# A hybrid state-space and delta-rule layer: four inverses around the GLU, an output projection in three parts, and high parts on ScalarE

## Chip, cores and metric

The kernel runs on one core of a Trainium2 chip. The metric is the device time of one execution in microseconds, the median of several runs.

## What is computed

One layer on 1024 latent tokens and 256 context tokens of width 1024. An input projection is split between two groups of heads. The S5 group is a two-way diagonal state-space scan with GELU, a GLU and a SiLU gate; the other is a gated delta rule with four heads of 128, in chunks of 64 tokens, both ways. Both are concatenated, projected, gated and normalised with the residual. Cut to what the change touches:

```python
h = x * (1.0 + scale[:, None]) + shift[:, None]
u, z_s5, qkv, z_gdn, beta_l, alpha_l = jnp.split(h @ p['w_in'], _proj_splits(), axis=-1)
...
g = jax.nn.gelu(y, approximate=False)                          # S5: y is the scan's read-out
s5 = g * jax.nn.sigmoid(g @ w_glu + b_glu) * jax.nn.silu(z)
...
sol = lax.linalg.triangular_solve(a_mat + eye, rhs, left_side=True, lower=True, unit_diagonal=True)
...
def step(s, inp):
    qi, ki, ui0, wi, qki, gi, gli = inp
    u = ui0 - wi @ s
    o = gi * (qi @ s) + qki @ u
    s = gli * s + ki.T @ u
    return s, o
...
y = jnp.concatenate([s5_lat, gdn_lat], axis=-1) @ w_out
x_new = _layer_norm(DEEPNORM_ALPHA * x + gate[:, None] * y, p['ln_g'], p['ln_b'])
```

## The kernel before

The kernel is written with tile pools and a list scheduler: the order in which the code is written gives priorities, and the scheduler settles, when the kernel is built, the order of the instructions on each engine. On the chip each engine goes through its own list in that order. A tile of a pool whose memory is still in use makes its first writer wait.

Matrices of float32 are multiplied in three passes (`mm3`, lines 140 to 143): both factors are split into a high and a low part, and low by high, high by low and high by high are added in PSUM. A 128x512 tile of a product of depth 128 is three matmuls. `split` (lines 874 to 876) makes the parts: ScalarE copies the high part, VectorE subtracts for the low one.

The work goes through these stages.

- Prologue (to about 90 us): the modulation from c and w_ada, h (tiles `h_hi`, `h_lo`, eight of 128x1024; `c_hi`, `c_lo` for the context) and the S5 input `u` (`u_mm`, line 499), with masks `lvm` for the inverse made on VectorE (line 1078).
- The projections of q, k and v with their convolutions, head by head, and beside them the S5 scan's states. Then a list written by hand, `ORD`, orders: eight z projections (`z0` to `z7`, 48 matmuls of 128x512 each, tiles `pjz`), four pairs of Toeplitz tiles (`t0` to `t3`), four read-outs (`y0` to `y3`: `y_stage`, tiles `py`, then transposes `pg` and the GELU tile `gT`), the GLU's weights (`w`) and the GLU (`g`: 96 matmuls `pgl`, then sigmoid on ScalarE, products on VectorE, stores to `d_mix`). `>y0` behind a name holds that item back until y0 is done.
- 20 inverses, for 4 heads in 5 batches of 256 tokens each (batch 4 is the context). `tbatch` builds one: decay sums `pd`, products `pkk`, the masked parts on GpSimd (`mg`, `dec`, `thi`, `tlo`, `xz`, `r`), a recursion of doubling block sizes in which TensorE (`pz`, `pp`, `px`), VectorE (`pad`, `xz`) and ScalarE alternate, and its result `pzz`. Its `finish` makes `zf` (ScalarE) and `ks` (GpSimd, from the load `kt`). Two of them are traced ahead of the others, next to the preparation of the first half of the output weights, `wo_a` (`load_wo`: load of a row `wor`, product with the gate on GpSimd or VectorE, split).
- For each head a scan of 10 chunk steps in both directions (`scan_head`, tiles `s`, `rr`, `uu`, `st`, sums in `acc`), then the gated norm.
- The output projection in two parts. `part_out` (heads of S5, k 0 to 3, 192 matmuls `poa`) is a generator; `fill` takes three matmuls of it at a time between the steps of an inverse or a scan. It adds alpha x and stores the sum in DRAM (`d_y`). When it is drained, after batch 16, `wo_b` is loaded into the memory of `wo_a`. `out_tile` then multiplies k 4 to 7 for each of 8 tiles of 128 tokens (192 matmuls `pout`), adds the stored sum (line 1553), and normalises: squares on ScalarE, scaling on VectorE (line 1568), the last addition on GpSimd or VectorE (lines 1570 to 1575). Tile `m7` is the part that comes from the last head's scan; the other three come back through DRAM (`load_mix`).

Loads and stores sit mostly on SP's queue, in order; some stores are issued by ScalarE.

## Time and profile before

| | |
|---|---|
| median of 3 runs | 914.95 us (912.2 to 919.06) |
| profiled execution | 909.83 us |
| its span, first to last instruction | 907.9 us |
| TensorE matmul busy, instructions | 808.6 us (89%), 6553 |
| VectorE busy | 681.8 us (75%), 1330 |
| ScalarE busy | 403.3 us (44%), 874 |
| GpSimd busy | 388.5 us (43%), 463 |

The profiled execution is one run; its 909.83 us hold the span of 907.9 and 1.9 us around it. In the rows PE is TensorE, DVE is VectorE, ACT is ScalarE, POOL is GpSimd, SP the queue that issues most loads; L and a number is a line of the kernel before. `x` and a number counts instructions. PEclk is the clock granted to TensorE as a share of its full speed. TensorE's matmuls overlap, so that a matmul shown with 0.39 us may start 0.23 us after the one ahead of it.

### The profile page before, as it was taken

The numbers are of one execution on the slowest core, as the hardware profiler recorded it, in microseconds if no ns is written. First come the engines' busy times: TensorE is split into PE (matmuls) and PEld (weight loads), VectorE is DVE, ScalarE is ACT, GpSimd is POOL, SyncE is SP. The second block draws the span as 40 slices with busy tenths as digits, with TensorE's granted clock in tenths as the row PEclk, the third lists the DMA queues.
The fourth block names the chain that finished last, engine by engine and source line by source line (L and its number), as shares of the span: only waits on it lengthen the run. The fifth ranks groups of instructions, "written<-read, shape, count | busy, mean of one in ns | idle before, by whom it ended". The sixth has DMA issues, their size and how long they took to land. (4 is left out here: it accounts for less than half of the span.)

```text
span 907.9 us, 17108 instructions
## 1 busy us (share of the span) xinstructions
PE 808.6 (89%) x6553; PEld 671.6 (74%) x6553; DVE 681.8 (75%) x1330; ACT 403.3 (44%) x874; POOL 388.5 (43%) x463
## 2 busy tenths in 40 slices
PE   4988999999897989999897894899989999888994
PEld 2756897787786668887786673688978887777883
DVE  7889986998877767998763389567685684775586
ACT  1232435234433344423433365566763573564363
POOL 3216240006999920001111078774963773351063
PEclk9989999999999999999898997799999999799998
DMA  9981547501314431444434477321234324324332
GB/s 246 302 157 49 196 158 232 152 24 47 133 47 157 128 122 47 134 131 137 138 115 123 147 263 228 127 83 59 64 118 149 118 92 158 110 77 150 111 127 105
DMA packets 120124, 119.48 MB, mean 132 GB/s; under 512 B 21406, under 2 KB 95702, under 8 KB 119914
## 3 DMA queue, kind: packets, MB, share of 16 engines
q1 hardware_dynamic: 101946, 85.42, 33.1%
...
q14 instruction: 31, 0.25, 0.1%
HBM read 81.33 MB, written 37.04 MB: 130 GB/s over the span
## 5 line engine op out<-in xcount | busy, mean ns | idle before, releaser
L713 POOL TENSOR_TENSOR rta<-ebuf,ar 128x64 f32<-128x64 f32 x38 | 25.9, 682 | 86.0 <-DVE ebuf L688 83.2
L846 POOL COPY hq<-ebuf 64x1024 f32<-64x1024 f32 x8 | 16.0, 2016 | 106.8 <-issue 60.6
L143 PE MATMUL pjz<-h_hi,wtz 128*128 128x512 f32 x128 | 51.5, 402 | 0.0
L141 PE MATMUL pjz<-h_hi,wtz 128*128 128x512 f32 x128 | 51.5, 402 | 0.0
L142 PE MATMUL pjz<-h_lo,wtz 128*128 128x512 f32 x128 | 51.4, 402 | 0.0
L1297 PEld LDWEIGHTS <-xz 128*128 128x128 f16 x480 | 37.4, 101 | 18.4 <-issue 12.1
L1186 POOL TENSOR_TENSOR mg<-tri,ghi 128x512 fp32r<-128x512 f32 x20 | 22.5, 1124 | 65.3 <-PE pd L1194 33.4
L1281 DVE TENSOR_TENSOR pad<-pp,lvm 128x256 f16<-128x256 f32 x100 | 40.7, 417 | 8.9 <-PE pp L1273 8.4
L1297 PE MATMUL px<-pad,xz 128*128 128x64 f16 x480 | 42.8, 197 | 4.8 <-DVE pad L1281 3.6
L1310 DVE TENSOR_TENSOR xz<-px,xz 128x512 f16<-128x512 f32 x60 | 40.6, 684 | 6.9 <-PE px L1297 6.5
L759 DVE SCALAR_TENSOR_TENSOR cav<-crv,cwt,cav 128x945 f32<-128x945 f32 (+2 forms) x32 | 39.6, 1238 | 6.0 <-ACT cav L749 5.5
L1297 PE MATMUL px<-xz,pad 128*128 128x64 f16 x480 | 43.0, 197 | 0.0
L759 DVE SCALAR_TENSOR_TENSOR cak<-crk,cwt,cak 128x945 f32<-128x945 f32 (+2 forms) x32 | 39.6, 1238 | 1.4 <-ACT cak L749 1.0
L759 DVE SCALAR_TENSOR_TENSOR caq<-crq,cwt,caq 128x945 f32<-128x945 f32 (+2 forms) x32 | 39.4, 1231 | 1.0 <-ACT caq L749 0.4
L1273 PE MATMUL pp<-xz,t 128*128 128x64 f16 x480 | 34.1, 198 | 6.7 <-DVE xz L1310 3.6
L821 ACT ACTIVATE csz<-pjz 128x512 f32<-128x512 f32 x16 | 9.4, 597 | 68.3 <-PE pjz L143 64.3
L1408 DVE SCALAR_TENSOR_TENSOR st<-st,gx,s 128x128 f32<-128x128 f32 x64 | 21.8, 342 | 21.9 <-PE s L1401 21.5
L1273 PEld LDWEIGHTS <-t 128*128 128x128 f16 x480 | 27.8, 102 | 10.5 <-issue 8.9
L1394 PE MATMUL s<-rr,zf 128*128 128x128 f32 x144 | 31.3, 303 | 4.1 <-DVE rr L1389 3.6
L1401 PE MATMUL s<-uu,ks 128*128 128x128 f32 x144 | 31.5, 302 | 2.6 <-ACT uu L1398 2.5
L1385 PE MATMUL s<-st,kT 128*128 128x128 f32 x144 | 30.8, 301 | 2.8 <-DVE st L1408 2.6
L1398 ACT ACTIVATE uu<-s 128x128 f32<-128x128 f32 x80 | 20.7, 276 | 26.5 <-PE s L1394 26.2
...
## 6 DMA issues: line engine op xcount, KB each, us to landing
...
```

The costliest lines, as they stand in the source:

```text
L141: T.matmul(ps, ll, rh, start=first, stop=False)
L142: T.matmul(ps, lh, rl, start=False, stop=False)
L143: return T.matmul(ps, lh, rh, start=False, stop=last)
L713: G.tensor_tensor(ta, prev, ar, op=ALU.mult)
L759: clast[typ, hd] = V.scalar_tensor_tensor(out=o, in0=rv[:, y0 + dy:y1 + dy, x0 + dx:x1 + dx], scalar=cwt[:, t, (dy + 1) * 3 + dx + 1:(dy + ...
L1273: T.matmul(pp[:, u * 64:(u + 1) * 64], t16[:, u, :], cols(xs[u], b, u // 2), start=True, stop=True)
L1281: V.tensor_tensor(scat(pad[:, 0, :], b, 256, 128 // b), pp[:, :256].rearrange("p (d n b) -> p d n b", d=2, b=b), lvm[:, l - 1].rearrange(" ...
L1297: ins = T.matmul(o, lt, rt, start=not on_act, stop=not on_act or w == 3 and i == 1)
L1310: V.tensor_tensor(xo, pxv, xo, op=ALU.add)
L1385: ins = T.matmul(p1_[:, :P], hs["kT"][:, ch, :], s0, start=True, stop=True)
L1394: ins = T.matmul(p2_[:, :P], hs["zf"][cp][:, d, i, :], rr, start=True, stop=True)
L1401: ins = T.matmul(p3_[:, :P], hs["ks"][cp][:, d, i, :], uu, start=True, stop=True)
```

## The change

Six edits, and what the scheduler makes of them.

1. `u_mm` goes over the four tiles pass by pass (high by low weight, high by high, low by high) where it took the three passes of one tile together.
2. The high parts `h_hi` and `c_hi` are copied by ScalarE (16 operations) where VectorE cast them; the 12 masks `lvm` are made by GpSimd.
3. In `ORD` all z projections stand ahead of y2 and y3. A new item `x` closes the pools of the projections and loads the first head; `b0` to `b3` are the first four inverses, traced from before the GLU's weights to behind the GLU. The last read-out's two tiles lie in a weight slot of their own.
4. The output projection has three parts: `part_out` as it was, `part_two` for heads 0 and 1 (k 4 and 5, 96 matmuls `pob`), which reads the first sum, adds and stores a second one, and `out_tile` for k 6 and 7 (96 matmuls `pout`).
5. The filler of part one starts with batch 4 (before: 2) at a rate of 1.0 (before: 0.8); it is drained after batch 14 (before: 16), where `wo_b` is loaded; then part two fills, and the last head's scan fills too, at 1.4 (before: not at all).
6. `m7` and the bias row `lnbb` lie in the inverse's pool.

```diff
     def u_mm(hf, k):
         wh, wl_ = (t[:, k % 2, :] for t in wu[k // 2])
-        for b in range(4):
-            s = 4 * hf + b
-            mm3(ups[hf][b], h_hi[k][:, s:LAT:8], h_lo[k][:, s:LAT:8], wh, wl_, k == 0, k == NK - 1)
+        for p, (h, w) in enumerate(((h_hi, wl_), (h_hi, wh), (h_lo, wh))):
+            for b in range(4):
+                T.matmul(
+                    ups[hf][b], h[k][:, 4 * hf + b:LAT:8], w, start=k == 0 and p == 0, stop=k == NK - 1 and p == 2,
+                )
...
-        V.tensor_copy(h_hi[k], raw[:, :LAT])
+        S.activation(h_hi[k], raw[:, :LAT], AF.Copy)
...
-        V.tensor_copy(c_hi[k], raw[:, LAT:])
+        S.activation(c_hi[k], raw[:, LAT:], AF.Copy)
...
-    d_y = tc.dram_tile([8, 2, P, 512], F32, name="d_y")
+    d_y = tc.dram_tile([2, 8, 2, P, 512], F32, name="d_y")
...
-        m8 = y4(f"m8_{ct}").rearrange("p (g f) -> p g f", g=8)
-        u8 = y4(f"u8_{ct}").rearrange("p (g f) -> p g f", g=8)
+        if ct < 3:
+            mu = [y4(f"m8_{ct}"), y4(f"u8_{ct}")]
+        else:
+            w8 = wslot(f"mu8_{ct}", F32)
+            mu = [w8[:, :1024], w8[:, 1024:]]
+        m8, u8 = (t.rearrange("p (g f) -> p g f", g=8) for t in mu)
...
         for d in range(2):
-            V.tensor_scalar(
+            G.tensor_scalar(
                 lvm[:, l - 1, d].rearrange("p c f -> p (c f)"), eq, half[:, d, l:l + 1], -1.0 / 2048,
...
-    ORD = "z0 z1 t0 z2 z3 t1 z4 y0 t2 z5>y0 y1 t3 z6>y1 y2 y3 w z7>y3 g"
+    ORD = "z0 z1 t0 z2 z3 t1 z4 z5 y0 t2 z6>y0 y1 t3 z7>y1 y2 y3 x b0 b1 w b2 g b3"
...
-            m7 = rp2.tile([P, 2, P], F32R, tag="m7", name=f"m7_{i}", bufs=4)
+            m7 = gt_.tile([P, 2, P], F32R, tag="thi", name=f"m7_{i}", bufs=4)
...
+    summed = set()
+
+    def part_two():
+        for tk in (3, 4, 2, 5, 1, 6, 0, 7):
+            yr = lp.tile([P, 2, 512], F32, tag="xr", name=f"yr{tk}", bufs=1)
+            Q.dma_start(yr, d_y[0, tk].rearrange("b p f -> p b f"))
+            mh, ml = load_mix(4, tk, 2)
+            for b in range(2):
+                sl = slice(b * 512, (b + 1) * 512)
+                ps = bankS(f"pob{tk}_{b}", "f")
+                for k in range(2):
+                    mm3(ps, mh[:, k, :], ml[:, k, :], wo(4 + k, 0, sl), wo(4 + k, 1, sl), k == 0, k == 1)
+                    if not k:
+                        yield
+                y1 = lp.tile([P, 512], F32, tag="y1", name=f"y2_{tk}_{b}", bufs=2)
+                V.tensor_tensor(y1, ps, yr[:, b, :], op=ALU.add)
+                Q.dma_start(d_y[1, tk, b], y1)
+                if b:
+                    summed.add(tk)
+                yield
...
     def out_tile(tk, m7):
...
-        mh, ml = load_mix(1, tk, 3)
+        while tk not in summed:
+            next(filler)
+        mh, ml = load_mix(6, tk, 1)
         for b in range(2):
...
-            Q.dma_start(yo, d_y[tk, b])
+            Q.dma_start(yo, d_y[1, tk, b])
             ps = bankO(f"pout{tk}_{b}")
-            for k in range(3):
-                mm3(ps, mh[:, k, :], ml[:, k, :], wo(4 + k, 0, sl), wo(4 + k, 1, sl), k == 0, False)
+            mm3(ps, mh[:, 0, :], ml[:, 0, :], wo(6, 0, sl), wo(6, 1, sl), True, False)
             mm3(ps, m7[:, 0], m7[:, 1], wo(7, 0, sl), wo(7, 1, sl), False, True)
...
-    RT, RS, NF = 0.8, 1.0, 64
+    RT, RS, NF = 1.0, 1.0, 64
...
-    hs = {0: head_prep(0)}
-    for si in range(NPAD):
-        mkpads(si)
-    fin = [tbatch(0, hs[0], CPS[n], n) for n in range(2)]
...
+            elif name == "x":
+                pY.close()
+                pH.close()
+                g1()
+                hs = {0: head_prep(0)}
+                for si in range(NPAD):
+                    mkpads(si)
+            elif name[0] == "b":
+                n = int(name[1])
+                fin.append(tbatch(0, hs[0], CPS[n], n))
...
-            if nb > 1:
+            if nb >= 4:
                 tbatch(hd, hs[hd], cp, nb % NS)()
             nb += 1
-            if nb == 4 * NS:
+            if nb == 14:
                 for _ in filler:
                     pass
+                filler, NF = part_two(), 200
...
-    scan_head(HEADS - 1, h3)
+    scan_head(HEADS - 1, h3, 1.4)
```

The scheduler's result at three places. On TensorE, behind the transposes of the GELU tile 3 (`pg3`), the kernel before starts the GLU and then runs z7 (`pjz13`):

```order
L863 MATMUL pg3_0_4677<-ident_64,ysb3_4630 128x128 x4
L863 MATMUL pg3_1_4683<-ident_64,ysb3_4630 128x128 x4
L141 MATMUL pgl0_0_4827<-g_hi0_4790,wgt0_4691 128x512
L141 MATMUL pgl1_0_4844<-g_hi0_4790,wgt1_4696 128x512
L141 MATMUL pjz13_0_4714<-h_hi0_243,wtz13_4711 128x512
L142 MATMUL pjz13_0_4714<-h_lo0_245,wtz13_4711 128x512
```

In the changed kernel z7 is long done, and steps of the first inverses (`pd0_4`, `pkk0_4`, `pd0_0`: head 0, batches 4 and 0) stand ahead of the last read-out (`py24`):

```order
L869 MATMUL pg2_0_4676<-ident_64,ysb2_4629 128x128 x4
L869 MATMUL pg2_1_4682<-ident_64,ysb2_4629 128x128 x4
L1178 MATMUL pd0_4_4778<-mg0_4_4775,trir_82 128x256 x4
L1197 MATMUL pkk0_4_4790<-kT_0_4759 128x128 x2
L1178 MATMUL pd0_0_4944<-mg0_0_4941,trir_82 128x256
L858 MATMUL py24_4703<-mu8_3_4690 128x128
L859 MATMUL py24_4703<-f6_4474,hq24_4700 128x128
```

So inverse steps went from behind the GLU's first half to ahead of the last read-out. On GpSimd, before, the five `ks` products of the first head stand ahead of the masks `xz` of batches 3 and 1:

```order
L1361 TENSOR_TENSOR ks0_2_5984<-kt_0_5367,gx_1099 128x512
L1237 AFFINE_SELECT xz0_3_5409<-mb0_3_5410 128x2x256
L1252 AFFINE_SELECT tlo0_3_5419<-tlo0_3_5419 128x512
L1246 AFFINE_SELECT thi0_1_5616<-t160_1_5606 128x512
L1251 TENSOR_TENSOR tlo0_1_5620<-tt0_1_5604,t160_1_5606 128x512
L1237 AFFINE_SELECT xz0_1_5610<-mb0_1_5611 128x2x256
```

In the changed kernel the `xz` of batch 1 is ahead of the `wor` rows, and the masks `r160` of batches 0 and 3, which an inverse needs near its end, stand behind the `ks` products (the one of batch 1 seven rows further on):

```order
L1221 AFFINE_SELECT xz0_1_5510<-mb0_1_5511 128x2x256
L1475 TENSOR_TENSOR wor1_5665<-wor1_5665,gate0_5655 128x512
L1475 TENSOR_TENSOR wor2_5673<-wor2_5673,gate0_5655 128x512
L1475 TENSOR_TENSOR wor3_5681<-wor3_5681,gate0_5655 128x512
L1305 AFFINE_SELECT r160_4_4925<-r160_4_4925 128x512
L1345 TENSOR_TENSOR ks0_4_5712<-kt_0_5706,gx_1099 128x512
...
L1345 TENSOR_TENSOR ks0_2_5944<-kt_0_5706,gx_1099 128x512
...
L1305 AFFINE_SELECT r160_0_5095<-r160_0_5095 128x512
L1331 TENSOR_TENSOR qg0_2_5938<-qg0_2_5938,qT_0_4760 128x512
L1305 AFFINE_SELECT r160_3_5285<-r160_3_5285 128x512
```

What waited for `kt` before was the start of batches 3 and 1; now it is the end of batches 0, 3 and 1. At the end, on TensorE, the kernel before starts the closing matmuls (`pout`) right behind the last inverse (`pzz3_2`), between scan steps (`s23`, `s33`, `s43`):

```order
L1336 MATMUL pzz3_2_9938<-xz3_2_9807,i1k_79 128x256
L1394 MATMUL s23_0_5_10111<-rr3_0_5_10109,zf3_1_9777 128x128
L1394 MATMUL s23_1_4_10095<-rr3_1_4_10093,zf3_2_9955 128x128
L1401 MATMUL s33_1_4_10099<-uu3_1_4_10097,ks3_2_9957 128x128
L1416 MATMUL s43_1_4_10103<-uu3_1_4_10097,pt3_2_9805 128x128
L141 MATMUL pout3_0_10281<-wo_b_9204,ml3_1_10275 128x512
```

In the changed kernel part two (`pob`) fills the scan, and the first closing matmul comes behind the scan's last step (`s43_1_9`):

```order
L143 MATMUL pob0_1_9875<-wo_b_8508,mh0_4_9827 128x512
L1399 MATMUL s43_1_9_10466<-st3_1_8_10440,qg3_0_9541 128x128
L1400 MATMUL s43_1_9_10466<-uu3_1_9_10464,pt3_0_9351 128x128
L141 MATMUL pob7_0_9924<-wo_b_8508,ml7_4_9920 128x512
...
L141 MATMUL pout3_0_10492<-wo_b_8508,ml3_6_10486 128x512
```

All 96 closing matmuls, and on VectorE all 16 additions of their sums, moved behind the last step of the scan, where 8 of the 16 additions stood before.

## Rows read from the trace of the kernel before

**Rows 1.** The page, the span in 40 equal slices of 22.7 us, TensorE.

```profile
PE   4988999999897989999897894899989999888994
```

**Rows 2.** Windows: us, busy of PE, PEld, DVE, ACT, POOL (x instructions), PEclk, DMA share, GB/s.

```profile
480.00:500.00 20.00, 13.43 (x106) 12.90 (x102) 5.80 (x9) 8.66 (x10) 3.94 (x2) 0.83 0.52 144
500.00:520.00 20.00, 15.63 (x69) 12.35 (x68) 6.39 (x9) 6.23 (x10) 0.00 (x0) 0.91 0.44 151
...
540.00:560.00 20.00, 13.42 (x93) 10.77 (x93) 18.03 (x20) 12.51 (x25) 16.87 (x16) 0.83 0.50 168
560.00:580.00 20.00, 11.36 (x152) 9.39 (x151) 15.46 (x27) 7.71 (x16) 19.70 (x21) 0.66 0.79 255
```

**Rows 3.** What TensorE waited for: us in total, times, longest us.

```profile
PE py L852 <- DMA d_g<-gT: 5.8, 1, 5.8
...
PE u L141 <- DVE h_lo L562: 3.8, 4, 1.6
```

**Rows 4.** Timeline, 507 to 630 us: start, us, engine, line, operation [idle before <-releaser].

```profile
507.10 0.79 PE L141 MATMUL pjz<-h_hi,wtz 128*128 128x512 f32 x1
...
519.76 0.39 PE L142 MATMUL pgl<-g_lo,wgt 128*128 128x512 f32 x1
...
519.99 0.39 PE L143 MATMUL pgl<-g_hi,wgt 128*128 128x512 f32 x1
...
545.69 0.40 PE L143 MATMUL pgl<-g_hi,wgt 128*128 128x512 f32 x1
...
555.67 0.33 SPq L1168 DMA_DIRECT2D kt<-d_kt  x1
...
564.30 6.33 POOL L1361 TENSOR_TENSOR ks<-kt,gx 128x512 f32<-128x512 f32 x5
...
587.59 0.61 PE L1394 MATMUL s<-vt,zf 128*128 128x128 f32 x4
...
629.36 0.38 PE L1336 MATMUL pzz<-xz,i1k 128*128 128x256 f16 x2
```

**Rows 5.** Windows of the last 130 us, columns as in rows 2.

```profile
780.00:800.00 20.00, 15.07 (x119) 12.75 (x117) 19.18 (x37) 10.16 (x24) 9.20 (x10) 0.74 0.20 61
800.00:820.00 20.00, 19.20 (x259) 17.76 (x259) 14.42 (x41) 13.64 (x46) 9.95 (x11) 0.91 0.39 113
820.00:840.00 20.00, 17.73 (x159) 15.32 (x156) 9.60 (x28) 9.93 (x29) 1.64 (x3) 0.91 0.43 138
...
860.00:880.00 20.00, 20.00 (x98) 16.57 (x97) 17.66 (x49) 13.16 (x37) 10.45 (x11) 1.00 0.30 97
```

**Rows 6.** Groups on VectorE, 865 to 908 us: xcount, busy us, mean ns, idle before.

```profile
L1568 DVE SCALAR_TENSOR_TENSOR yo<-yo,st,lngg 128x512 f32<-128x512 f32 x14 | 14.3, 1021 | 1.9 <-ACT xs L1559 1.7
...
L1553 DVE SCALAR_TENSOR_TENSOR yo<-pout,yo 128x512 f32<-128x512 f32 x12 | 7.9, 683 | 0.8 <-PE pout L143 0.8
...
L1570 DVE SCALAR_TENSOR_TENSOR yo<-yo,st,lnbb 128x512 f32<-128x512 f32 x4 | 3.0, 752 | 2.0 <-POOL st L1564 1.9
...
L1562 DVE TENSOR_SCALAR st<-st 128x1 f32<-128x1 f32 x7 | 1.4, 205 | 0.0
```

**Rows 7.** Timeline: last part of the last inverse, last scan sum, VectorE's last operation.

```profile
831.68 0.38 PE L1336 MATMUL pzz<-xz,i1k 128*128 128x256 f16 x2
...
874.48 0.28 DVE L1419 TENSOR_TENSOR acc<-s,acc 128x128 f32<-128x128 f32 x1
...
901.91 0.75 DVE L1570 SCALAR_TENSOR_TENSOR yo<-yo,st,lnbb 128x512 f32<-128x512 f32 x1 [0.73 <-POOL st L1564]
```

**Rows 8.** Groups of the first 90 us, VectorE's and ScalarE's, and one window (columns as in rows 2).

```profile
L560 DVE CAST h_hi<-hraw 128x1024 fp32r<-128x1024 f32 x8 | 7.8, 977 | 2.0 <-ACT hraw L556 1.9
...
L1078 DVE TENSOR_SCALAR lvm<-eq,half 128x128 bf16<-128x128 f32 x12 | 5.1, 458 | 0.2
...
L495 ACT ACTIVATE wu<-wur 128x1024 fp32r<-128x1024 f32 x4 | 4.2, 1058 | 23.2 <-DMA wur<-in_w_in_dram 17.9 <-DMA dt<-in_s_log_dt_dram 5.3
...
20.00:40.00 20.00, 18.92 (x155) 13.35 (x154) 17.45 (x75) 5.19 (x8) 2.39 (x1) 1.00 1.15 304
```

More of the change, by code (lines that the diff above doesn't have):

```diff
@@ L1118, in tile_hybrid_block @@
     zs_ = [(g, ct) for g in range(2) for ct in range(4)]
-    gps, gts, rps = ExitStack(), ExitStack(), ExitStack()
+    gps = ExitStack()
     def g1():
-        nonlocal gp, gt_, psT, rp
+        nonlocal gp, gt_, psT
         gp = gps.enter_context(tc.tile_pool(name="gp", bufs=2))
-        rp = gps.enter_context(tc.tile_pool(name="rp", bufs=1))
-        gt_ = gts.enter_context(tc.tile_pool(name="gt", bufs=1))
+        gt_ = gps.enter_context(tc.tile_pool(name="gt", bufs=1))
         psT = gps.enter_context(tc.tile_pool(name="psT", bufs=1, space=PSUM))
@@ L1129, in tile_hybrid_block @@
     marks = {}
-    for st in ORD.split():
-        name, _, hold = st.partition(">")
-        with ExitStack() as hx:
-            if hold:
-                hx.enter_context(tc.issue_after(marks[hold].ins))
-            if name[0] == "z":
-                z_tile(*zs_[int(name[1])])
-            elif name[0] == "t":
-                s5_toeplitz(2 * int(name[1]), 2 * int(name[1]) + 2)
-            elif name[0] == "y":
-                marks[name] = y_stage(int(name[1]))
-            elif name == "w":
-                glu_weights()
-            elif name == "g":
-                pY.close()
-                pH.close()
-                ep_.close()
-                glp = pW.enter_context(tc.tile_pool(name="glp", bufs=1, side="right"))
-                g1()
-                glu_stage()
     ACTL = (1, 3)
@@ L1501, in tile_hybrid_block, with load_mix @@
     YT = iter("pt pt ks zf qg ks zf pt ks zf qg ks zf pt ks zf".split())
-    def load_mix(b, tk, nk):
-        mh = lp.tile([P, 4, P], F32R, tag="mh", name=f"mh{tk}_{b}", bufs=2)
-        ml = lp.tile([P, 4, P], F32R, tag="ml", name=f"ml{tk}_{b}", bufs=2)
+    def load_mix(k0, tk, nk):
+        mh = lp.tile([P, 4, P], F32R, tag="mh", name=f"mh{tk}_{k0}", bufs=2)
+        ml = lp.tile([P, 4, P], F32R, tag="ml", name=f"ml{tk}_{k0}", bufs=2)
         raw = ml[:, :nk].bitcast(F32)
-        Q.dma_start(raw, d_mix[4 * b:4 * b + nk, :, tk * P:(tk + 1) * P].rearrange("k p t -> p k t"))
+        Q.dma_start(raw, d_mix[k0:k0 + nk, :, tk * P:(tk + 1) * P].rearrange("k p t -> p k t"))
         split(mh[:, :nk], ml[:, :nk], raw)
@@ L1524, in part_out @@
                 V.scalar_tensor_tensor(out=y1, in0=xr[:, sl], scalar=ALPHA, in1=ps, op0=ALU.mult, op1=ALU.add)
-                S.dma_start(d_y[tk, b], y1)
+                S.dma_start(d_y[0, tk, b], y1)
+                yield
[17 more added lines that the diff above has]
+                    summed.add(tk)
                 yield
@@ L1529, in tile_hybrid_block, with fill @@
     fl = [0.0, 0]
-    def fill(ins, rate, lim=64):
+    def fill(ins, rate, lim=200):
         if fl[1] >= lim:
@@ L1589, in mkpads @@
             V.memset(pd_, 0.0)
-    hs = {0: head_prep(0)}
-    for si in range(NPAD):
-        mkpads(si)
-    fin = [tbatch(0, hs[0], CPS[n], n) for n in range(2)]
+    fin = []
+    for st in ORD.split():
+        name, _, hold = st.partition(">")
+        with ExitStack() as hx:
+            if hold:
+                hx.enter_context(tc.issue_after(marks[hold].ins))
+            if name[0] == "z":
+                z_tile(*zs_[int(name[1])])
+            elif name[0] == "t":
+                s5_toeplitz(2 * int(name[1]), 2 * int(name[1]) + 2)
+            elif name[0] == "y":
+                marks[name] = y_stage(int(name[1]))
+            elif name == "w":
+                glu_weights()
+            elif name == "g":
+                ep_.close()
+                glp = pW.enter_context(tc.tile_pool(name="glp", bufs=1, side="right"))
+                rp = gps.enter_context(tc.tile_pool(name="rp", bufs=1))
+                glu_stage()
+            elif name == "x":
[8 more added lines that the diff above has]
+                fin.append(tbatch(0, hs[0], CPS[n], n))
     wos.append(rp.tile([P, 2, 4, D], F32R, tag="wo", name="wo_a"))
@@ L1625, in tile_hybrid_block @@
             head_out(hd, hs[hd])
-    gts.close()
-    rp2 = rps.enter_context(tc.tile_pool(name="rp2", bufs=1))
     nO = [0]
@@ L1634, in tile_hybrid_block @@
     lngg = gs.tile([P, D], F32, tag="vt", name="lngg", bufs=2)
-    lnbb = rp2.tile([P, D], F32, name="lnbb")
+    lnbb = gt_.tile([P, D], F32, tag="mg", name="lnbb", bufs=1)
     Q.dma_start(lngg, ln_g.to_broadcast([P, D]))
@@ L1645, in tile_hybrid_block @@
         dbg(locals())
-    rps.close()
     gps.close()
```

## Prediction

> **What bounds the kernel now.** I read the slices first, then windows where the slices dip, then the waits of TensorE, then single rows. The slices show TensorE near full almost everywhere [rows 1]; the dips are the first slice, slices 22 to 26 (477 to 590 us) and the last. So the kernel is bound by TensorE, and what can be gained is where TensorE stands or runs at the low clock. In the four windows 480 to 520 and 540 to 580 it is idle for 6.6 + 4.4 + 6.6 + 8.6 = 26 us [rows 2]. The granted clock there is 0.83, 0.91, 0.83 and 0.66, means of the two levels 2.4 and 1.2 GHz; a busy time of 13.42 at 0.83 holds 0.17 x 13.42 = 2.3 us of loss, and all four hold 2.3 + 1.4 + 2.3 + 3.9 = 10. Some 36 us are lost between the last Toeplitz tile and the first four inverses. The reader should see in rows 2 that VectorE is idle in the first two windows (5.8 and 6.4 of 20) and nearly full in the third (18.0), GpSimd full in the fourth (19.7): the GLU, the wo_a preparation and the first inverses come one after the other, each with another engine as its limit.
>
> A second stretch, 780 to 840, holds 4.9 + 0.8 + 2.3 = 8 us of idle time and 3.9 + 1.7 + 1.6 = 7 of low clock [rows 5]: wo_b is being prepared (VectorE 19.2 of 20), and then the last head's scan runs without cover. From 855 TensorE is full again, and the run ends 13 us after its last matmul.
>
> **1. The inverses around the GLU.** Before, z7 stands between the read-outs and the GLU: 48 matmuls from 507.10 to 519.76, 12.7 us [rows 4]. It covers the splitting of the GLU's input. After, z6 and z7 stand ahead of t3, so every later step starts 12.7 us later and its cover is gone; what stands there instead are five matmuls of 128x256 and two of 128x128 of the first inverses, about 1 us if a column costs what it does in the GLU. So the wait of 5.8 us of the last read-out for its loads [rows 3] keeps about 5. The edit that gives y3 its own slot lets the u8 load go early, but order shows the m8 load still behind the store of the convolution kernel, and its last piece behind the store of gT2: I count nothing for it. I take the start of the GLU proper as unchanged, 519. It has 94 matmuls at 0.23 (519.76 to 519.99 is the spacing, [rows 4]), 22 us, and the order puts 8 us of inverse steps between them; before, with 2 us of such steps, the stretch lasted to 546.1 [rows 4] and so lost 2.3. After: 519 + 22 + 8 + 2.3 = 551.
>
> What comes next decides. The load kt of the first head's keys takes memory that the GLU and the wor rows hold; kt was issued at 555.67, 9.6 us after the GLU's last matmul [rows 4], behind the GLU's last products. I take the same distance: kt at 561. GpSimd then finds five ks products at once (6.33 us, [rows 4]), and behind them, now, the masked r of batches 0, 3 and 1: 21 instructions from the first ks to r of batch 1, 6.3 + 16 x 0.94 (19.70 by 21, [rows 2]) = 21. With 5 us for the landing of kt, r of batch 1 is there at 561 + 5 + 21 = 587 (the first scan step, which waits for less, may come some 15 us ahead of the 587.59 it has now), and by the instructions in order 16 to 19 us of TensorE follow up to the end of the fifth inverse, batch 2: 606. Before, that end stood at 629.4 [rows 4]. That is 23 us, but by then the kernel before had done 48 fill matmuls of the output projection and the changed one 24: 24 x 0.23 = 5.6 us, and 1.4 of other work. **Net -16.** Bounds: with the 36 us wholly back, less what the covers above keep, -30; with GpSimd's queue as slow as in 560 to 580, +11 (rival B). I stay near the middle, by the chain of kt, whose rows I have.
>
> A page of the Trainium skill bears on this stretch. VectorE and GpSimd each take 18 to 20 us of 20 there [rows 2], and the same kind of operation on VectorE, 128x512 with two inputs, has a mean of 1.02 us in one group and 0.75 in another of the tail [rows 6]. "SBUF — State Buffer", section Who interferes with whom, says that a VectorE instruction with two SBUF inputs and a GpSimd instruction that reads SBUF exclude each other for their whole length. By that rule, more work side by side on these two engines gives less than the free slots suggest; by the rows alone the GLU's products would be hidden. The means above already hold that stretching, so the sum does not change; the tail, where it could, is rival C.
>
> **2. The prologue.** Sixteen casts leave VectorE: eight at 0.98 us, eight of a quarter of the size, taken at half of it; twelve masks at 0.46 go to GpSimd [rows 8]. That is 7.8 + 4 + 5.5 = 17 us less for VectorE, which is busy 17.45 of 20 in 20 to 40. ScalarE, at 5.2 of 20, takes a 128x1024 in 1.06 us [rows 8]: each chain becomes 0.1 longer. The new order of the passes of u lets them start without h_lo, whose waits sum to 3.8 us [rows 3]. But the DMA share is 1.15 in that window, so the weights set the pace: **-1.5**, bounds -7 (VectorE was the limit) and +3 (ScalarE's own scale-and-shift queued behind its copies).
>
> **3. The second filler.** The 192 closing matmuls become 96 fill matmuls on heads 0 and 1 and 96 at the end. Order puts 42 of the 96 ahead of the last inverse, 42 x 0.23 = 9.8 us more work there, into holes of 15 us of which the wo_b preparation holds about half (VectorE at 19.2 of 20 cannot be helped by matmuls). I let 6.4 fall into holes: **+3.4**. Bounds 0 and +10. The sixteen extra sums (0.68 each, [rows 6]) and sixteen extra stores lie in 800 to 850, where VectorE is busy 9.6 to 14 of 20 [rows 5]. The filler of part one runs from batch 4 on, with a higher rate: same matmuls in the same stretch, nothing, bounds -5 and +4.
>
> **4. From the last inverse to the last scan sum.** Before, 831.7 to 874.5, 42.8 us [rows 7], with 96 closing matmuls (22 us) in between. After, 42 fill matmuls: 54 x 0.23 = 12.4 less. The fill is there from the start, so that the idle 2.3 and the low clock's 1.6 of 820 to 840 [rows 5] mostly go, 4 more: 26.4 are left, **-16.4**. Bounds: -22 if all 22 us were pure delay, -8 if the chain of the scan (TensorE, VectorE, ScalarE in turn) takes up half of what TensorE no longer has to do.
>
> **5. The end.** Before, 33.4 us pass from the last scan sum to the end of the span, and VectorE has 8 of the 16 half-tile sums left. After, all 16 are left. VectorE then has 16 x 1.02 (scaling) + 16 x 0.68 (sums) + 4 x 0.75 + 24 small ones at 0.2 [rows 6] + 28 of 128x128 at 0.3 (the 0.28 of [rows 7]) = 16.3 + 10.9 + 3.0 + 4.8 + 8.4 = 43.4. TensorE has only 22 us. VectorE becomes the limit: 43.4, 1 to get the first tile through, and the 5.2 that the last output takes after VectorE (902.7 to 907.9) make 50. **+16.5**, bounds +8 (the 1.02 falls to 0.75) and +24 (rival C).
>
> Sum: -16 - 1.5 + 3.4 - 16.4 + 16.5 = -14. The span of 907.9 becomes 893.9, the profiled execution of 909.83 becomes 895.8. The runs shown have a median of 914.95, 0.56% above the profiled one; with the same ratio that is 900.8. I take 899, since term 1 has a little more room below than above. A measurement of this kernel can tell about 1% from no change.
>
> **Rivals.**
> A. The inverses pay in full: kt lands while the fourth inverse still has VectorE steps to do, and the r operations are not late. Term 1 is -30, and the fill matmuls fit the holes, term 3 is 0: 17.4 less, 882 for the median. For it: TensorE is idle 26 us in that stretch and the work is there. Against: ks stands ahead of r in GpSimd's order.
> B. Slower: kt becomes the gate of all four inverses. TensorE goes in order, and with kt late, r of batch 0, then 3 and 1 are late one for one, with three scan steps ahead of them. Every us of kt after 561 is a us of the end. With kt at 587 the time is 899 + 26 = 925, slower by 1.1%; that is where it decides. For it: VectorE had 18 of 20 for 40 us there and now has the inverses' steps among the GLU's products; GpSimd has 19.7 of 20. Against: 26 us later than before would need the GLU to end near 577, when its matmuls and the steps between them sum to 30.
> C. The end is stretched: all 16 scalings meet GpSimd's additions and take 1.5 (twice 0.75) where I took 1.02. 16 x 0.48 = 7.7: 907. The rule of the Trainium skill named above would give this; the rows show it for part of them.
> D. The change does not do what it says: the GLU's steps on VectorE and the inverses' add up, and the stretch 480 to 630 takes what it took. Term 1 is 0: 915.
>
> **How the numbers follow.** Forecast 0.45, A 0.25, B 0.12, C 0.13, D 0.05. Faster by over 1% (below 905.8): most of the forecast, A, in all 0.67. Within 1%: C, D and the upper edge of the forecast, 0.20. Slower: B, 0.13. The range takes in A and C and D, and leaves out the far end of A and most of B: 874 to 921. The forecast's own range is 891 to 907.
>
> **What would show it.** Right: the GLU's last matmul near 551, kt issued near 561, the fifth inverse done near 606, the last inverse near 818, the last scan sum near 844, VectorE over 90% busy from there on and TensorE idle for half of that time. Wrong: an idle TensorE of more than 15 us before the r operations (B), a last inverse before 805 (A), a tail from the last scan sum of under 40 us or over 56 us, or a prologue that moves by more than 5 us.

## The result: 950.77 us, slower by 3.8%

The changed kernel has a median of 950.77 us (947.68 to 961.94), the kernel before 914.25 on the same chip: 1.038 times the time before, with a 95% interval of 1.0322 to 1.0439. The forecast was 899.

The profiled execution took 961.94 us, 11 us more than the median, at a mean granted clock of 0.936 where the three others had 0.947 to 0.950, so all stretches below hold a share of that and the size of an effect is read from the medians. TensorE's slices of the kernel after (24.0 us each) stand against [rows 1]:

```profile
PE   5989999998989899999996886988989987788782
```

Slices 22 and 25 (504 to 528 and 576 to 600 us) dip around the GLU and the first inverses, as slices 22 to 26 did before; new is the end, which reads 8 7 7 8 8 7 8 2 from slice 33 (768 us) on. The timeline of the kernel after has the points of [rows 4, 7]: the GLU's last matmul, kt, the end of the fifth and of the last inverse, the last scan sum.

```profile
567.66 0.40 PE L143 MATMUL pgl<-g_hi,wgt 128*128 128x512 f32 x1
...
573.72 0.33 SPq L1152 DMA_DIRECT2D kt<-d_kt  x1
...
628.61 0.64 PE L1320 MATMUL pzz<-xz,i1k 128*128 128x256 f16 x2
...
872.30 0.38 PE L1320 MATMUL pzz<-xz,i1k 128*128 128x256 f16 x2
...
905.24 0.28 DVE L1403 TENSOR_TENSOR acc<-s,acc 128x128 f32<-128x128 f32 x1
```

The first z matmul starts at 376.0 after and at 370.2 before. The difference of the spans, 959.6 - 907.9 = 51.7 us, falls into these pieces:

| stretch | before | after | difference |
|---|---|---|---|
| start to first z matmul | 370.2 | 376.0 | +5.8 |
| to the end of the fifth inverse | 259.2 | 252.6 | -6.6 |
| to the end of the last inverse | 202.3 | 243.7 | **+41.4** |
| to the last scan sum | 42.8 | 32.9 | -9.9 |
| to the end of the span | 33.4 | 54.4 | **+21.0** |

So most of the time went between the fifth and the last inverse, where scans, inverses, the preparation of wo_b and the filler run, and half as much behind the last scan sum. The waits from 575 us to the end (in all, times, longest), first of the kernel after, then of before, name what stood there:

```profile
ACT mh L881 <- DMA ml<-d_mix: 36.0, 17, 5.3
...
DVE ml L882 <- ACT mh L881: 21.5, 14, 5.0
...
DVE y L1508 <- DMA xr<-in_x_dram: 13.9, 5, 6.0
...
DVE y L1527 <- DMA yr<-d_y: 11.8, 5, 4.1
...
PE pob L141 <- DVE y L1527: 8.8, 6, 3.2
...
PE poa L141 <- DVE y L1508: 6.2, 3, 2.9
```

```profile
ACT mh L875 <- DMA ml<-d_mix: 9.0, 11, 1.6
...
DVE ml L876 <- ACT mh L875: 6.2, 4, 2.3
...
DVE y L1524 <- DMA xr<-in_x_dram: 4.0, 1, 4.0
...
PE poa L141 <- DVE y L1524: 2.0, 1, 2.0
```

The loads are the filler's own (the last eight of `ml` are the final stage's). VectorE works through its list in order, so while it waits for a row of x (xr), a stored sum (yr) or a split (ml), the next `pad`, `xz` or `rr` of an inverse or a scan stands behind it. It stood 21.5 + 13.9 + 11.8 = 47.2 us for them after and 10.2 before. Of these waits, 27.4 us after and 5.2 before lie between the fifth and the last inverse. TensorE, which has its list too, in turn stood 8.8 + 6.2 = 15.0 us in front of matmuls of the filler (`pob`, `poa`) until VectorE had made the sum ahead of them, and 2.0 before. That the difference of 37 us on VectorE is near the loss of 36.5 proves nothing yet.

The last windows (columns as in [rows 2]) and VectorE's groups from 905 us on:

```profile
860.00:880.00 20.00, 16.53 (x111) 13.61 (x110) 7.25 (x18) 6.44 (x19) 0.63 (x1) 0.94 0.63 213
880.00:900.00 20.00, 18.77 (x113) 15.90 (x112) 11.28 (x36) 5.90 (x25) 1.41 (x2) 0.97 0.66 207
900.00:920.00 20.00, 13.09 (x49) 9.58 (x50) 7.62 (x24) 3.25 (x14) 1.39 (x2) 0.91 0.56 180
920.00:940.00 20.00, 17.12 (x75) 13.05 (x73) 19.53 (x60) 13.65 (x35) 10.80 (x9) 1.00 0.18 66
940.00:960.00 20.00, 1.85 (x7) 1.05 (x6) 13.51 (x30) 8.34 (x18) 14.12 (x12) 0.65 0.42 158
```

```profile
L1574 DVE SCALAR_TENSOR_TENSOR yo<-yo,st,lngg 128x512 f32<-128x512 f32 x16 | 15.9, 994 | 0.4 <-ACT xs L1565 0.4
L1559 DVE SCALAR_TENSOR_TENSOR yo<-pout,yo 128x512 f32<-128x512 f32 x16 | 10.7, 680 | 0.3 <-POOL yo L1581 0.3
L1576 DVE SCALAR_TENSOR_TENSOR yo<-yo,st,lnbb 128x512 f32<-128x512 f32 x4 | 3.6, 927 | 0.4 <-POOL st L1570 0.4
```

Where 860 to 880 had TensorE and VectorE nearly full [rows 5], VectorE now works 7 to 11 us of 20 up to 920, and the whole final stage comes behind that.

### The profile page after: what moved, and what is told of

It reads as the page before. It is cut to its first block, busy times and chain, and to the rows that moved or that the text cites. A ratio compares the mean times of both kernels' runs of the same rounds, so it can differ in the third digit from the quotient of the medians.

```text
span 959.6 us, 17236 instructions
## 1 busy us (share of the span) xinstructions
PE 836.5 (87%) x6553; PEld 688.3 (72%) x6553; DVE 681.2 (71%) x1326; ACT 417.4 (43%) x896; POOL 395.1 (41%) x475
## 4 chain that ended last, share of the span: by engine, by line
PE 45%; DMA 17%; DVE 15%; POOL 13%; issue 4%; ACT 3%; SPq 2%; POOLq 0%; DVEq 0%; ACTq 0%
DMA xr<-in_x_dram 4%; DMA yr<-d_y 3%; PE pjz L143 3%; PE pjz L142 3%; POOL rta L717 3%; PE u L503 3%; PE pjz L141 3%; POOL rta L715 3%; POOL ebuf L718 3%; POOL rtb L716 2%; PE ph L646 2%; PE px L1281 2%; DMA wur<-in_w_in_dram 1%; PE poa L141 1%; PE pba L570 1%
## 5 line engine op out<-in xcount | busy, mean ns | idle before, releaser
L1265 DVE TENSOR_TENSOR pad<-pp,lvm 128x256 f16<-128x256 f32 x100 | 40.6, 416 | 15.5 <-PE pp L1257 15.2
L1281 PE MATMUL px<-pad,xz 128*128 128x64 f16 x480 | 41.6, 197 | 10.9 <-DVE pad L1265 5.6
L1257 PE MATMUL pp<-xz,t 128*128 128x64 f16 x480 | 33.5, 196 | 9.6 <-DVE xz L1294 4.6
L1170 POOL TENSOR_TENSOR mg<-tri,ghi 128x512 fp32r<-128x512 f32 x20 | 21.8, 1088 | 48.5 <-PE pd L1178 48.2
L761 DVE SCALAR_TENSOR_TENSOR cak<-crk,cwt,cak 128x945 f32<-128x945 f32 (+2 forms) x32 | 39.6, 1238 | 2.1 <-ACT cak L751 1.7
L503 PE MATMUL u<-wu,h_hi 128*128 128x512 f32 x128 | 38.9, 438 | 0.0
L1378 PE MATMUL s<-rr,zf 128*128 128x128 f32 x144 | 32.5, 312 | 2.6 <-ACT zf L1343 1.5
L1292 ACT ACTIVATE xz<-px 128x512 f16<-128x512 f32 x40 | 23.8, 594 | 24.3 <-PE px L1281 17.6
L1385 PE MATMUL s<-uu,ks 128*128 128x128 f32 x144 | 33.1, 317 | 0.9 <-ACT uu L1382 0.4
L1369 PE MATMUL s<-st,kT 128*128 128x128 f32 x144 | 33.3, 320 | 0.7 <-DVE st L1390 0.6
```

The costliest lines, as they stand in the source:

```text
L503: T.matmul(ups[hf][b], h[k][:, 4 * hf + b:LAT:8], w, start=k == 0 and p == 0, stop=k == NK - 1 and p == 2,)
L761: clast[typ, hd] = V.scalar_tensor_tensor(out=o, in0=rv[:, y0 + dy:y1 + dy, x0 + dx:x1 + dx], scalar=cwt[:, t, (dy + 1) * 3 + dx + 1:(dy + ...
L1257: T.matmul(pp[:, u * 64:(u + 1) * 64], t16[:, u, :], cols(xs[u], b, u // 2), start=True, stop=True)
L1265: V.tensor_tensor(scat(pad[:, 0, :], b, 256, 128 // b), pp[:, :256].rearrange("p (d n b) -> p d n b", d=2, b=b), lvm[:, l - 1].rearrange(" ...
L1281: ins = T.matmul(o, lt, rt, start=not on_act, stop=not on_act or w == 3 and i == 1)
L1369: ins = T.matmul(p1_[:, :P], hs["kT"][:, ch, :], s0, start=True, stop=True)
```

## The experiments

Ratios are to the kernel before, run on the same chip, with their 95% intervals. The theories in the expectations are numbered as they came up; each text says what its theory holds.

**Which part costs it.** Edits 1 and 2 alone; edit 3 alone (with edit 6 and the filler's later start, which come with it); edits 4 and 5 alone (the filler starting with batch 2, as before):

```diff
-        V.tensor_copy(h_hi[k], raw[:, :LAT])
+        S.activation(h_hi[k], raw[:, :LAT], AF.Copy)
```

> The kernel before with edits 1 and 2 alone (passes of u over four tiles, high parts on ScalarE, masks on GpSimd). Theory 1 (the loads of the fill, one row deep, hold VectorE and so TensorE): these edits are not the cause; the changed kernel's first z projection started 5.8 us later than before (376.0 against 370.2), so at most that, ratio 1.000 to 1.007. Theory 2 (the inverses around the GLU cost the time): the same, as this part holds neither. Theory 3 (ScalarE's copies delay the front): ratio above 1.007.

0.9981 [0.9949, 1.0013]: nothing.

```diff
-    ORD = "z0 z1 t0 z2 z3 t1 z4 y0 t2 z5>y0 y1 t3 z6>y1 y2 y3 w z7>y3 g"
+    ORD = "z0 z1 t0 z2 z3 t1 z4 z5 y0 t2 z6>y0 y1 t3 z7>y1 y2 y3 x b0 b1 w b2 g b3"
...
-            if nb > 1:
+            if nb >= 4:
```

> The kernel before with edit 3 alone (order of z and read-outs, the slot of y3, four inverses around the GLU; the fill can start only with batch 4; two-part projection). Theory 1: this part neither wins nor loses much: the fifth inverse ended at 628.6 in the changed kernel against 629.4, with 5.8 us of that from the front and 5.6 us of fill still to do, so ratio 0.992 to 1.005. Theory 2: it loses, ratio above 1.015.

1.013 [1.0077, 1.0183], between the two ranges: a loss, where a gain was the point. VectorE waits 9.5 us for xr and 31.7 us behind splits.

```diff
-    RT, RS, NF = 0.8, 1.0, 64
+    RT, RS, NF = 1.0, 1.0, 64
...
-            if nb == 4 * NS:
+            if nb == 14:
                 for _ in filler:
                     pass
+                filler, NF = part_two(), 200
```

> The kernel before with edits 4 and 5 alone (three-part projection, fill rates, wo_b after batch 14, fill in the last scan). Theory 1: this part holds nearly the whole loss: 30 to 40 us between the fifth inverse and the end, ratio 1.030 to 1.042, with VectorE waiting more than 15 us for the loads xr and yr. Theory 2: ratio under 1.015.

1.0379 [1.0314, 1.0444]: the projection alone holds as much as the whole change, so the parts do not add up (1.3 and 3.8%, and 3.8 together). VectorE waits 12.9 us for yr here and 1.3 for xr, just under the 15 that were expected.

**Rows in halves.** xr and yr come as 128x1024 in one buffer: the load of the next row cannot start before the last addition from the one before it. Two halves in two buffers take the same memory (the gate row of `wo_b`, which uses this buffer too, comes in halves as well):

```diff
-            yr = lp.tile([P, 2, 512], F32, tag="xr", name=f"yr{tk}", bufs=1)
-            Q.dma_start(yr, d_y[0, tk].rearrange("b p f -> p b f"))
+            yrs = []
+            for b in range(2):
+                yrs.append(lp.tile([P, 512], F32, tag="xr", name=f"yr{tk}_{b}", bufs=2))
+                Q.dma_start(yrs[b], d_y[0, tk, b])
```

> The changed kernel with the rows xr and yr loaded as two halves of their own, in the same memory, so that each half is loaded again as soon as its own sum is done. Theory 1: the next first half is loaded some 3 to 4 us earlier and the waits of VectorE for xr and yr (13.9 and 11.8 us) about halve: ratio to before 1.020 to 1.028, 10 to 17 us under the changed kernel. Theory 2: no change beyond 4 us, 1.034 to 1.042.

1.0133 [1.0075, 1.0191], 930.76 us: 20 us come back, and the loss falls from 3.8 to 1.3%, more than theory 1 expected. The issues of the kernel after, 575 to 920 us (count, KB, us to landing), and of this run, 575 to 875:

```profile
xr<-in_x_dram SPq DMA_DIRECT2D x8, 512.0 KB, 5.3
...
yr<-d_y SPq DMA_DIRECT2D x8, 512.0 KB, 4.3
```

```profile
xr<-in_x_dram SPq DMA_DIRECT2D x16, 256.0 KB, 3.5
...
yr<-d_y SPq DMA_DIRECT2D x16, 256.0 KB, 3.4
```

and the waits of this run from 575 us on, with none for xr and none of `poa` for VectorE left:

```profile
ACT mh L881 <- DMA ml<-d_mix: 31.8, 19, 5.2
...
DVE ml L882 <- ACT mh L881: 22.0, 14, 3.9
...
PE pob L141 <- DVE y L1534: 4.0, 4, 2.2
DVE y L1534 <- DMA yr<-d_y: 4.0, 2, 3.8
```

The fifth to the last inverse takes 221.9 us here (628.52 to 850.40), 21.8 less than after: most of what comes back comes from the stretch named above. The scheduler made a new order with the edit (54 of part two's matmuls run ahead of the last inverse, where 42 did), so smaller loads, a second buffer and the new order are not told apart.

**The split's load one tile ahead.**

```diff
-            mh, ml = load_mix(4, tk, 2)
+            mh, ml = split_raw(*nxt)
+            if n2 < 7:
+                nxt = load_raw(4, order2[n2 + 1], 2)
```

> The changed kernel with half rows (as e4) and with the other load of the fill, the mixed heads in ml, issued one tile ahead of its split. In the changed kernel ScalarE stood 36.0 us in front of splits whose load had not landed and VectorE 21.5 us behind it; in e4 still 31.8 and 22.0. Theory 1 (the fill's loads hold the engines): both fall under 10 us and the time falls by another 12 to 22 us, ratio to before 0.990 to 1.001. Theory 4 (what costs is the place of the fill, dense in the later batches and the last scan, not its loads): ratio stays at 1.008 to 1.018, as in e4.

1.0117 [1.0079, 1.0154]. The waits for ml hardly fall (ScalarE 27.6, VectorE 20.1 us), so this run does not say what they cost. The same two edits (half rows and the load ahead) were added to edit 3, to edits 4 and 5, and to the kernel before:

> e2 (edit 3 alone) with half rows and the load one tile ahead. In e2 VectorE waited 31.7 us behind splits and 9.5 us for xr. Theory 1: these waits go and with them 12 to 20 us, ratio 0.991 to 1.000, so that the inverses around the GLU were worth something all along. Theory 4: the fill starts at batch 4 and ends at 833 where it ended at 773, and wo_b with it; ratio stays at 1.008 to 1.018. Theory 2 (the inverses themselves cost): the same as theory 4.

1.0017 [0.9987, 1.0048], just above theory 1's range, where edit 3 alone had 1.013.

> e3 (edits 4 and 5 alone) with half rows and the load one tile ahead. Theory 1: 1.038 falls to 1.005 to 1.015. Theory 4: 1.02 to 1.03, half rows alone taking what they took in e4.

1.0105 [1.0065, 1.0146], where the projection alone had 1.0379. ScalarE's waits for ml fell here too, from 36.2 to 19.4 us.

> The kernel before with half rows and the load one tile ahead, nothing else. There ScalarE waited 9.0 us, VectorE 6.2 and 4.0 us for these loads. Theory 1: at most 5 to 10 us are to be had, ratio 0.990 to 0.999. Theory 4: nothing, 0.998 to 1.004.

0.9915 [0.9882, 0.9948], 910.58 us: the best kernel here, and it has none of the change. Its waits for ml are no shorter than before (ScalarE 11.3 us); its profiled execution took 911.7 us against 909.83, so the profile does not show where the 0.85% is.

**The early drain, and the inverses with half rows.**

```diff
-            if nb == 14:
+            if nb == 4 * NS:
```

> e4 (the changed kernel with half rows) with part one of the fill drained after batch 16, as before, where the change drains it after batch 14. In e5 the drain ran from 752 to 780 without an inverse ending, and the next inverse ended at 789. Theory 5 (the early drain takes the fill from the inverses and leaves them bare): ratio falls from 1.013 to 0.995 to 1.005. Theory 6 (the third part itself costs: 16 more sums and splits, loads and stores): ratio 1.008 to 1.018.

1.0134 [1.006, 1.0208] against 1.0133: where the drain stands makes no difference that can be measured; theory 5 falls.

```diff
-    RT, RS, NF = 0.8, 1.0, 64
+    RT, RS, NF = 1.0, 1.0, 64
```

> Edit 3 alone with half rows and a fill rate of 1.0 (e2 and e6 had 0.8 and their fill ended at 833 and 825, against 773). Theory 4 (the inverses around the GLU leave the fill too late): with the rate 1.0 the fill ends near 785 and the ratio falls to 0.985 to 0.995, under the 0.9915 of e8. Theory 2 (the inverses themselves cost): 0.999 to 1.008.

0.9977 [0.9939, 1.0015], between the ranges: with rows that come in time the inverses around the GLU cost nothing and bring nothing that can be measured.

**What is left of the projection.** Three parts with half rows, the old rate of 0.8 and the late drain; beside it edits 1 and 2 with half rows and two parts:

> The three-part projection alone with half rows, with the fill's rate and the drain as before (0.8, batch 16). Theory 5: 0.985 to 0.997, at or under e8. Theory 6: 1.003 to 1.012, near e7 (1.0105).

> The kernel before with edits 1 and 2 and half rows, without the load ahead. If half rows alone make the gain of e8 and the front is neutral: 0.988 to 0.995. If the load ahead made it: 0.996 to 1.001.

1.0192 [1.0133, 1.0251], above both ranges, and 0.9976 [0.994, 1.0012]: without the load ahead, half rows gave the old filler nothing that can be measured. Up to the end of the last inverse (839.3 and 836.7) and the last scan step (878.4 and 879.0) the two profiles stand level; from there to the end the three parts need 58.9 us, the two parts 33.5. Windows of the run with three parts, then of that with two (columns as in [rows 2]):

```profile
840.00:850.00 10.00, 8.66 (x50) 6.99 (x48) 4.35 (x11) 2.03 (x7) 0.00 (x0) 1.00 0.99 319
...
870.00:880.00 10.00, 7.76 (x33) 6.39 (x34) 4.37 (x12) 2.65 (x12) 0.70 (x1) 0.83 0.64 202
880.00:890.00 10.00, 5.95 (x24) 3.80 (x22) 2.64 (x6) 1.19 (x5) 0.70 (x1) 1.00 0.77 229
...
900.00:910.00 10.00, 7.20 (x31) 5.05 (x30) 10.00 (x29) 8.24 (x21) 6.57 (x6) 1.00 0.22 78
```

```profile
840.00:850.00 10.00, 9.11 (x47) 7.59 (x47) 2.47 (x6) 2.35 (x7) 0.00 (x0) 1.00 0.39 134
...
870.00:880.00 10.00, 10.00 (x49) 8.29 (x48) 6.75 (x19) 6.57 (x16) 6.05 (x7) 1.00 0.36 126
880.00:890.00 10.00, 10.00 (x47) 8.18 (x46) 9.88 (x23) 5.23 (x15) 5.85 (x6) 1.00 0.43 144
```

With two parts TensorE is full from 870 to 890, and normalising (GpSimd 6 of 10) is under way by 870. With three, the DMA share is 0.99 against 0.39 at 840, TensorE is idle 1 to 4 us of 10 up to 890, and then VectorE alone is full. Two causes offered themselves for the starved fill: the order in SP's queue, where a load of a finished sum (yo) stands until its store has landed, with the next loads behind it (16.6 us in 12 waits from 835 us on), as at 867.75 here:

```profile
866.02 0.45 SPq L1551 DMA_DIRECT2D d_y<-y  x1
866.56 0.38 SPq L1540 DMA_DIRECT2D yr<-d_y  x1
867.75 3.21 SPq L1578 DMA_DIRECT2D yo<-d_y  x2
871.48 0.32 SPq L1551 DMA_DIRECT2D d_y<-y  x1
```

or the bytes, 8.4 MB more (one more load and one more store of a sum of 4.2 MB).

```diff
-            Q.dma_start(yo, d_y[1, tk, b])
+            G.dma_start(yo, d_y[1, tk, b])
```

> The three-part projection alone with half rows and the late drain, as the run at 1.0192, with one thing changed: the final stage's loads of the row sums (yo, 16 of them) are issued by GpSimd's queue and no longer stand in SyncE's. Theory 8 (SyncE's queue works in order; a load of a sum waits there until the store of that sum has landed, and the next tile's store and the next loads of the fill stand behind it): ratio 0.998 to 1.008, and the stretch from the last scan step to the end falls from 58.9 us to 35 to 48. Theory 7 (the bytes: rows loaded, stored and loaded again share the DMA engines' rate): ratio 1.012 to 1.023, that stretch above 52 us.

1.0143 [1.0094, 1.0191], 55.2 us behind the last scan step: theory 7's ranges.

```diff
-            Q.dma_start(yo, d_y[1, tk, b])
+            Q.dma_start(yo, d_y[0, tk, b])
```

> The three-part projection alone with half rows and the late drain, as the run at 1.0192, but the final stage loads the sum that part one stored, not part two's, so the output lacks part two's contribution; the loads stay in SyncE's queue, with the same number of bytes, and none waits for a fresh store. Theory 8 (waiting for the fresh store at the head of the queue): ratio 0.998 to 1.008. Theory 7 (bytes): ratio 1.012 to 1.023. If this falls and the run with the other queue does not, the wait for the store itself sets the end, wherever it stands.

1.0115 [1.0072, 1.0158], 55.7 us: between the ranges in time, and not the 35 to 48 us that theory 8 wanted behind the scan.

> The changed kernel with half rows (which stood at 1.0133) and the loads of the row sums on GpSimd's queue. Theory 8: ratio 0.995 to 1.006. Theory 7: ratio 1.009 to 1.017, as without the edit.

1.0118 [1.0068, 1.0167] against 1.0133: the queue is not what costs the 1.3%, and theory 8 falls. A small share for the waiting loads is not excluded (1.0115 against 1.0192).

```diff
-                Q.dma_start(yrs[b], d_y[0, tk, b])
+                Q.dma_start(yrs[b][:, :128], d_y[0, tk, b, :, :128])
...
-                Q.dma_start(d_y[1, tk, b], y1)
+                Q.dma_start(d_y[1, tk, b, :, :128], y1[:, :128])
...
-            Q.dma_start(yo, d_y[1, tk, b])
+            Q.dma_start(yo[:, 384:], d_y[1, tk, b, :, :128])
```

> The three-part projection alone with half rows and the late drain, as the run at 1.0192, with the same number of DMAs in the same queue, but a quarter of the bytes in three of them: part two loads 128 columns of 512 of a sum and adds them four times over, stores 128 columns of its own sum, and the final stage loads 128 columns. So three quarters of each sum are wrong columns of the output and 9.4 MB less is moved. Theory 7 (bytes through the DMA engines): ratio 0.998 to 1.008, the stretch from the last scan step to the end 34 to 46 us against 58.9. Theory 8 (order in SyncE's queue, waits for a store to land, with the time of a small DMA nearly that of a large one): ratio 1.011 to 1.019, that stretch above 50 us.

1.0172 [1.0086, 1.0257]. The issues of 830 to 895 us, first with whole sums (the run at 1.0192), then with a quarter:

```profile
yo<-d_y SPq DMA_DIRECT2D x16, 256.0 KB, 3.8
yr<-d_y SPq DMA_DIRECT2D x14, 256.0 KB, 4.3
```

```profile
yo<-d_y SPq DMA_DIRECT2D x16, 64.0 KB, 1.8
yr<-d_y SPq DMA_DIRECT2D x14, 64.0 KB, 2.0
```

These loads land in half the time, and 55.8 us still pass behind the last scan step: theory 7 falls too. Both numbers lie in theory 8's ranges, which the runs before had ruled out: neither theory is left. Windows of this run:

```profile
850.00:860.00 10.00, 9.60 (x55) 7.93 (x54) 5.55 (x18) 3.10 (x13) 0.71 (x1) 1.00 0.34 92
...
890.00:900.00 10.00, 7.30 (x30) 4.82 (x29) 10.00 (x27) 7.45 (x19) 8.28 (x7) 1.00 0.31 116
...
910.00:920.00 10.00, 0.00 (x0) 0.00 (x0) 8.89 (x15) 3.58 (x10) 6.88 (x6) 0.51 0.44 166
```

Here the fill is better fed, the scan ends earlier (34.3 us behind the last inverse, 42.3 with two parts), and the final stage of all eight tiles, VectorE's, follows it: -8.0 + 22.3 = +14 us behind the last inverse, on a span of 925. That is a cost of three parts that the loads of the sums do not explain. The waits for ml are there still (ScalarE 29.0, VectorE 13.6 us from 575 us on).

> The changed kernel with half rows (1.0133) and the same quarter of the bytes of the sums in part two's load and store and the final stage's load; three quarters of each sum are wrong columns. Theory 7: ratio 0.994 to 1.004, so that nothing of the changed kernel's loss is left once its rows come in time and its sums cost a quarter. Theory 8: 1.009 to 1.016.

1.0081 [1.0049, 1.0113], 925.48 us: between the ranges, 5 us less than with whole sums, and the two intervals overlap.

**The front on top of the best.**

> The kernel before with the changed kernel's front (high parts by ScalarE, masks), half rows and the load ahead. If the front is worth nothing or 0.2%, as in the runs at 0.9981 and 0.9976: ratio 0.987 to 0.993. If front and filler edits get in each other's way: 0.995 to 1.002.

0.994 [0.9905, 0.9976], just between the ranges and not told apart from 0.9915: the front adds nothing.

## Why the prediction was wrong

**Term 3 failed: "same matmuls in the same stretch, nothing, bounds -5 and +4"** for part one's filler, and +3.4 for part two. I costed the filler by its matmuls and VectorE operations and never by its loads. The last inverse was to be 212 us behind the fifth (606 to 818) and came 243.7 behind it. The windows of that stretch, after, before, and with half rows (columns as in [rows 2]):

```profile
628.60:872.30 243.70, 217.08 (x2246) 190.86 (x2244) 154.68 (x356) 121.70 (x354) 112.80 (x136) 0.93 0.35 112
```

```profile
629.40:831.70 202.30, 187.01 (x2129) 167.37 (x2127) 140.75 (x337) 116.73 (x345) 111.99 (x136) 0.97 0.35 110
```

```profile
628.52:850.40 221.88, 205.82 (x2256) 181.84 (x2254) 155.60 (x359) 121.95 (x354) 110.49 (x136) 0.98 0.41 130
```

TensorE's idle time was to shrink, by 6.4 us of fill in holes; it grew from 15.3 to 26.6 us. The granted clock, a mean of its two levels of 2.4 and 1.2 GHz, was 0.93 where it had been 0.97: 0.07 x 217 = 15 us of the busy time are loss, and 0.03 x 187 = 6 before. The other 20 us of the 41.4 are work, 117 more matmuls: 66 of the filler's and 51 that ran ahead of the fifth inverse before. One edit to the loads brought the idle time back to 16.1 us and the clock to 0.98, 21.8 us in these profiles. Part of the clock's share may belong to the profiled execution alone, so the size goes by the medians: 20 us, 3.8% down to 1.3. That the filler's loads made that part of the loss is shown: VectorE's waits for xr and TensorE's for the sums (`poa`) went with the edit, and half rows with the load ahead brought edit 3 alone from 1.013 to 1.0017 and the projection alone from 1.0379 to 1.0105. A share of the scheduler's new order in it is not excluded.

With half rows the stretch is still 9.9 us over the 212. Its idle time is that of before (16.1 and 15.3), so the fill fell into no holes: the 6.4 us, with 12 more matmuls of part two (12 x 0.23 = 2.8), make 9.2, an estimate. Of the 1.3% that stay in the whole kernel, a quarter of the sums' bytes takes off 0.5, which the intervals do not tell from nothing; the rest was not taken apart. What the longer waits for ml cost stays open, since no run of the whole change brought ScalarE's under 25 us.

Three small slips change nothing: 42 x 0.23 is 9.7 and not 9.8; 43.4 + 1 + 5.2 is 49.6; and of the "18 to 20 us of 20" for VectorE and GpSimd, [rows 2] show 15.5 and 18.0, 16.9 and 19.7.

**Term 1, -16, was about 0.** The fifth inverse ended 252.6 us after the first z matmul, where before it took 259.2: -6.6, with 24 fill matmuls (5.6 us) and 51 others less done by then, which leaves no gain. kt came at 573.7 and not at 561: the GLU's matmuls ended 191.7 us after the first z matmul (175.5 before, and the forecast's 551 is 181 behind the 370.2 of before). From 480 to 570 us TensorE waited 6.0 us for `pad` of VectorE and 4.5 for `dec` of ScalarE, steps of the inverses that now stand among the GLU's matmuls. From kt to the fifth inverse 54.9 us passed, where 45 were forecast. The runs at 0.9977 and 1.0017 agree. This is rival D's price for the term, and close to D's mechanism; it lies inside the bounds of -30 and +11. Windows from the first z matmul to the end of the fifth inverse, before and after (columns as in [rows 2]):

```profile
370.20:629.40 259.20, 226.13 (x2091) 187.00 (x2090) 185.12 (x282) 120.09 (x206) 96.23 (x95) 0.93 0.45 142
```

```profile
376.00:628.60 252.60, 220.07 (x2016) 180.24 (x2015) 176.46 (x274) 115.92 (x200) 95.54 (x95) 0.93 0.46 142
```

TensorE is idle 33.1 us in the one and 32.5 in the other, at the same mean clock: the idle time moved and did not go, and what is shorter is the work, by 75 matmuls.

The wait of the last read-out for its loads was forecast at about 5 and is 4.4.

**Term 2, -1.5, cannot be told from 0** (0.9981 and 0.9976). The +5.8 in the table is not the change: the first z matmul starts anywhere from 369.7 to 378.9 in the profiled runs, with the old front and the new one.

**Term 4, -16.4, was -9.9** and inside its bounds: the matmuls left the stretch as counted (42 of the fill's run there), but TensorE's idle time, which was to go, grew from 2.9 to 6.9 us.

**Term 5, +16.5, was +21.0** and inside its bounds, its mechanism right in the main: VectorE is full from 920 to 940. It was to be over 90% busy from the last scan sum on and was busy 39.1 of 54.4 us. VectorE's three large groups were forecast at 16.3, 10.9 and 3.0 us and took 15.9, 10.7 and 3.6. The 4.4 over goes with part two, which ended at 913.8, 8.5 us behind the last scan sum. In the run at 1.0192 this term (+24.7), with a smaller term 4 (-2.9), makes most of the loss. Terms 4 and 5 pay for each other: in the two runs at 1.0133 and 1.0134 part two is done before the scan ends (871.9 and 874.9, against 889.1 and 885.3), the end is short (39.1 and 39.6 us behind the last scan step) and the scan late; in the run at 1.0172 it is the other way round. That VectorE's 16 extra sums (11.0 us in each run) are what is left is argued from the windows; a run without them was not made.

**Rival C** (all 16 scalings at 1.5 us) fell: their mean is 0.994. In the run at 1.0192 they read, shortest/median/longest in ns:

```profile
L1597 DVE SCALAR_TENSOR_TENSOR yo<-yo,st,lngg x16: 733/740/1648, 897.9 to 929.4; 128x512 f32<-128x512 f32 x16
```

The long ones are those that begin while an addition of GpSimd runs, as here:

```profile
911.66 1.44 POOL L1604 TENSOR_TENSOR yo<-yo,lnbb 128x512 f32<-128x512 f32 x1 [0.83 <-ACT yo L1603]
912.00 1.65 DVE L1597 SCALAR_TENSOR_TENSOR yo<-yo,st,lngg 128x512 f32<-128x512 f32 x1
```

In this run they are 3 of 16 (1.34 to 1.65 us), in the kernel after 6 of 16 (1.01 to 1.82); all others take 0.73 to 0.75, those included that begin first and have an addition begin beside them. One exception, in the kernel after, began 0.1 us before the recorded end of an addition and took 0.73. The Trainium skill, "SBUF — State Buffer", Who interferes with whom, has a VectorE instruction with two SBUF inputs and a GpSimd instruction that reads SBUF contend for an exclusive lock; the trace agrees with it in these numbers. What the rival had wrong is the count: not all 16 met an addition that was running. **Rival B**, the one that was slower, fell too: kt was 12.7 us late, but from 570 to 630 us TensorE waits 0.3 us for an r, and its longest wait there is 4.0 us, for a `pad` of ScalarE. None of the rivals had the filler's loads.
